# Residual addition from PSUM, and the first ConvFFN weights prepared ahead through DRAM

## The chip, the cores and the metric

The kernel runs on one NeuronCore of a Trainium2 chip. The time is the device time of one execution in microseconds (us). Of several runs the median is given. The profile is of one further execution, and its times count from the first instruction.

## The reference

One layer of a diffusion backbone over 1024 latent tokens and 256 context tokens, 1024 features, all in float32:

```python
hx = modulate(rms_norm(x, norm_pre_mix[l]), sh1, sc1)
fx, ox, zx, gtx, _ = mixer_core(hx, ctx_states, w_in[l], conv_qkv[l], a_log[l], dt_bias[l])
yx = merge_branches(fx, ox, zx, gtx, dn_norm[l], w_fourier[l], w_dn[l], w_out[l])
x = x + gt1 * rms_norm(yx, norm_post_mix[l])
x = ffn_sublayer(x, sh2, sc2, gt2, norm_pre_ffn[l], norm_post_ffn[l], w_up[l],
                 conv_ffn[l], w_down[l], rows, GRID_W)
...
def merge_branches(f_in, o_dn, z, gates, dn_norm, w_fourier, w_dn, w_out):
    ...
    y_f = fourier_mix(f_in) @ w_fourier
    y_d = o @ w_dn
    return (gates[:, :, 0] * y_f + gates[:, :, 1] * y_d) @ w_out

def ffn_sublayer(stream, shift, scale, gate, g_pre, g_post, w_up, conv_w, w_down, rows, cols):
    h = modulate(rms_norm(stream, g_pre), shift, scale)
    a, u = jnp.split(h @ w_up, 2, axis=-1)
    a = dwconv2d(a, conv_w, rows, cols)
    y = (jax.nn.silu(a) * u) @ w_down
    return stream + gate * rms_norm(y, g_post)
```

The change touches the weights of `w_up` and the addition `x + gt1 * rms_norm(yx, ...)`.

## The kernel before

Every float32 product is three matmuls of rounded halves: each operand is split into a rounded part h and a rest l, and h·h, h·l and l·h are summed in PSUM. To split a weight, ScalarE rounds it to h, and VectorE (or, for ConvFFN's weights, POOL) subtracts h from it, which gives l.

The order of the instructions is not that of the source. All operations are recorded, and a list scheduler (`Program.schedule`) sets for each engine and for SP's DMA queue the order of issue, from estimated costs, the longest path behind an operation, and the buffers that its tiles lie in. Every instruction is issued by one helper line, L349. Each engine then goes through its own list in order. A tile waits until the last use of whatever lay in its place before.

The stages around the change, in the times of the profile before:

- Up to 1050, the gates' projection; from there to about 1150 the delta branch's output projection (`for k in range(KT)` over `a["wd"][k]`, 8 steps of 48 matmuls). The weights of a step are two halves of 128x512 (`h_d00`, `h_d0512` and so on), loaded by SP, rounded by ScalarE and split by VectorE. In the same stretch SP loads the last modulation weights (`in_w_ada`).
- To 1201, the Fourier branch's projection, which merges both branches into `mH` and `mL`.
- To about 1300, the output projection by token tiles of 128 rows, the last three of them (5, 6, 7) together. For each tile `root` computes the norm's factor (squares on ScalarE, a power of one column on POOL), `post` scales the two PSUM banks `y2[g]` and adds them to the residual `res`, the sum is stored (`x1d`), normed again and transposed to the hidden state `hh`.
- `side_b` and `sum_b`: ConvFFN's up projection is a scheme of seven products in place of eight over halves of tokens and features. Its moving sides are sums, differences or copies of four parts of `hh`, 28 tiles, each rounded on ScalarE and split on VectorE.
- From 1290 to 1740, the 22 column pairs of the up projection (a pair c has the 128 columns of a and the 128 of u). `both(c)` loads four raw weight halves of 256 KB, makes five sums or differences of them on POOL (`summed`), takes two as they are (`split_w`), and splits all seven: 7 products m1 to m7 of 12 matmuls each. The pools of `wq` hold 5 tiles h, 5 tiles l and 8 raw ones. Products of pairs 0 and 1 are interleaved by a list, later pairs follow one after the other. A pair's result goes into a padded buffer (`apad`, cleared by POOL once), through the 3x3 convolution on VectorE, and to DRAM.
- From 1740, the down projection.

Of the kernel before, what the change touches and what calls it, by code (L numbers as in the profile page):

```python
# [9 lines left out]
F32 = mybir.dt.float32  # L10
# [6 lines left out]
P = 128  # L17
# [470 lines left out]
def layer(prog, a, out):  # L488
# [824 lines left out]
    def m_tile(p_, name, dtype=F32R):  # L1313
        return p_.tile([P, HALF], dtype, tag="m", name=name)
# [55 lines left out]
    def modulation(i):  # L1370
# [8 lines left out]
        for g in range(2):  # L1379
# [11 lines left out]
            else:  # L1391
# [6 lines left out]
                else:  # L1398
                    ve.scalar_tensor_tensor(mod2[:, o0:o0 + 4], pq, 1.0, gpre[:, 8 + g * 4:12 + g * 4],
                                            op0=ALU.add, op1=ALU.mult)  # L1400

    mf = [[m_tile(mp[g], f"mf{k}{g}", F32) for g in range(2)] for k in range(KT)]
    for k in range(KT):
        wl = weights(a["wd"][k], f"d{k}")

        def used(g, hs, pt):
            gl = yt.tile([P, HALF], F32, tag="gl", name=f"g1l{k}{g}")
            sp.dma_start(gl, gd[1, k, :, hs])
            ve.scalar_tensor_tensor(mf[k][g], gl, 1.0, pt, op0=ALU.add, op1=ALU.mult)
        proj_rows(wl, half_rows(oz), f"d{k}", used)  # L1410
        if k % 2:
            modulation(2 + k // 2)
    close(yt)
    close(ozp)

# [48 lines left out]
    def post(y2, res, grow_, name, pl):  # L1464
        r = root(y2, name, pl)
        for g in range(2):
            hs = slice(g * HALF, (g + 1) * HALF)
            t_ = pl.tile([P, HALF], F32, tag="pt", name=f"pt_{name}{g}")
            ve.scalar_tensor_tensor(t_, y2[g], r, grow_[:, hs], op0=ALU.mult, op1=ALU.mult)
            ve.tensor_tensor(res[:, hs], res[:, hs], t_, op=ALU.add)  # L1470


    rings = {1: (mp[0], mp[0]), 3: (lp[0], lp[0]), 4: (mp[1], mp[1]), 2: (lp[1], lp[1])}
# [110 lines left out]

    def both(c):
        raw = {}
        for n, (key, at) in enumerate((("u0", 0), ("u1", 1), ("a0", 0), ("a1", 1))):
            raw[key] = wq.tile([P, HALF], F32, tag="r", name=f"r{key}_{c}", bufs=RAW)
            sp.dma_start(raw[key], a["wu"][c + (NC_FF if key[0] == "u" else 0)][:, at * HALF:(at + 1) * HALF])

        def summed(x_, y_, op, name):
            s_ = wq.tile([P, HALF], F32, tag="l", name=f"qs_{name}{c}", bufs=WL)
            po.tensor_tensor(s_, raw[x_], raw[y_], op=op)
            return split_w(s_, f"{name}{c}")
# [5 lines left out]
        ap_ = apad[c % 2]  # L1600
        inner = lambda g: ap_[:, 1 + 8 * g:9 + 8 * g, 1:GW + 1]
        grid = lambda t_: t_.rearrange("p (a b) -> p a b", b=GW)
        def step(m):
            if m == 2:
                chain(A, summed("u0", "u1", ALU.add, "m2"), 1, True)
                first(lambda: se.activation(v_, A, AF.Copy, scale=-1.0))
            elif m == 5:
                chain(B, summed("a0", "a1", ALU.add, "m5"), 4, True)
                first(lambda: ve.tensor_tensor(v_, v_, B, op=ALU.subtract))
            elif m == 1:  # L1610
                chain(C, summed("a0", "u1", ALU.add, "m1"), 0, True)
                first(lambda: ve.tensor_tensor(v_, v_, C, op=ALU.add))
            elif m == 4:
                chain(A, split_w(raw["u1"], f"m4{c}", True), 3, False)
                first(lambda: se.activation(u_[:, 0:HALF], A, AF.Copy))
            elif m == 3:
                chain(B, split_w(raw["a0"], f"m3{c}", True), 2, False)
                first(lambda: se.activation(inner(1), grid(B), AF.Copy))
            elif m == 7:
                chain(A, summed("a1", "u1", ALU.subtract, "m7"), 6, False)  # L1620
                ve.tensor_tensor(inner(0), grid(A), grid(v_), op=ALU.add)
            else:
                chain(B, summed("u0", "a0", ALU.subtract, "m6"), 5, False)
                ve.tensor_tensor(u_[:, HALF:T], B, v_, op=ALU.add)
# [173 lines left out]
```

## Time and profile before

| | |
|---|---|
| median of 3 runs | 2006.71 us (2005.4 to 2008.88) |
| profiled execution | 2007.74 us |
| its span | 2006.0 us |
| TensorE busy | 1947.3 us, 97% |
| VectorE busy | 1388.3 us, 69% |
| ScalarE busy | 829.7 us, 41% |
| POOL busy | 565.0 us, 28% |
| mean granted TensorE clock | 0.991 |

A row of the profile names the engine (PE is TensorE, PEld its weight loads, DVE VectorE, ACT ScalarE, SPq SP's queue), the operation and its operands: p is PSUM, m SBUF, d DRAM, and in_wu_dram is the input `w_up`; fp32r is the rounded type. Idle time stands with what ended it. A group's mean is over all its instructions.

### The profile page before, as it was taken

Reading aid. Unit: us, or ns where it says so; the run is one execution under the profiler, and the core shown is the slowest. Engines: PE = TensorE matmul, PEld = TensorE weight load, DVE = VectorE, ACT = ScalarE, POOL = GpSimd, SP = SyncE. Lnnn points to the kernel's source line nnn. Section 1 sums busy time; section 2 is a strip of 40 time slices with the busy share of each in tenths; the row PEclk is TensorE's granted clock in tenths of the full one; section 3 lists DMA queues with packets and bytes.
Section 4 is the critical chain, followed back from the end, with each engine's and each line's share of the span. In section 5 each row is a group of like instructions: output and inputs, shape, how many; then the busy total and the mean of one; then the engine's idle time right before and its main releaser. Section 6 shows DMA issues by size and latency. Waiting matters only on the chain.

```text
span 2006.0 us, 31360 instructions
## 1 busy us (share of the span) xinstructions
PE 1947.3 (97%) x11470; PEld 1562.6 (78%) x11470; DVE 1388.3 (69%) x2868; ACT 829.7 (41%) x1948; POOL 565.0 (28%) x573
## 2 busy tenths in 40 slices
PE   7999999999999999999999999989999999999998
PEld 3878888787788887888777778757788888778876
DVE  5659687788678768754656483589988989873132
ACT  5575446455345355333431132444444344622121
POOL 3120121202111122011211000457788888500000
PEclk9999999999999999999999999989999999999999
DMA  7153352544345254233778561312222222543131
GB/s 304 53 193 103 101 156 69 151 142 149 87 135 155 59 168 149 67 104 103 252 254 282 182 216 45 116 44 87 87 83 85 84 75 84 196 156 122 57 126 53
DMA packets 180636, 257.51 MB, mean 128 GB/s; under 512 B 75921, under 2 KB 97522, under 8 KB 180482
## 3 DMA queue, kind: packets, MB, share of 16 engines
q1 hardware_dynamic: 180482, 255.51, 39.5%
q8 instruction: 90, 1.47, 0.3%
q14 instruction: 64, 0.52, 0.1%
HBM read 194.52 MB, written 60.94 MB: 127 GB/s over the span
## 4 chain that ended last, share of the span: by engine, by line
PE 74%; DVE 11%; DMA 5%; ACT 4%; issue 2%; POOL 1%; SPq 0%; DVEq 0%; POOLq 0%; ACTq 0%
PE p L349 74%; DVE m L349 10%; ACT m L349 4%; DMA m<-d 2%; DMA d<-m 2%; DVE p L349 2%; POOL m L349 1%; DMA m<-in_wi_dram 1%; ACT p L349 1%; DMA m<-in_wu_dram 0%; DMA m<-in_w_ada_dram 0%; SPq L349 0%; ACT L349 0%; DVEq L1787 0%; POOLq L1787 0%
## 5 line engine op out<-in xcount | busy, mean ns | idle before, releaser
L349 PE MATMUL p<-m,m 128*128 128x512 f32 (+5 forms) x11310 | 1934.3, 336 | 49.1 <-DVE m L349 17.9
L349 PEld LDWEIGHTS p<-m,m 128*128 128x128 f32 (+3 forms) x11310 | 1544.4, 172 | 429.7 <-issue 53.7
L349 DVE TENSOR_TENSOR m<-m,m 128x512 fp32r<-128x512 f32 (+27 forms) x1116 | 584.1, 539 | 242.6 <-ACT m L349 215.6
L349 ACT ACTIVATE m<-m 128x512 fp32r<-128x512 f32 (+8 forms) x669 | 430.5, 662 | 629.5 <-DMA m<-d 157.4
L349 POOL TENSOR_TENSOR m<-m,m 128x512 fp32r<-128x512 f32 (+5 forms) x338 | 449.8, 1353 | 832.4 <-DVE m L349 672.6
L349 ACT ACTIVATE m<-p 128x512 f32<-128x512 f32 (+4 forms) x510 | 220.9, 447 | 306.9 <-PE p L349 270.2
L349 DVE SCALAR_TENSOR_TENSOR m<-p,m,m 128x128 f32<-128x128 f32 (+4 forms) x488 | 204.0, 452 | 88.4 <-ACT m L349 38.5
L349 DVE SCALAR_TENSOR_TENSOR p<-m,m,p 128x512 f32<-128x512 f32 x352 | 240.1, 749 | 3.5 <-ACT p L349 1.2
L349 ACT ACTIVATE m<-p,m 128x128 f32<-128x128 f32 (+2 forms) x240 | 115.8, 495 | 183.1 <-PE p L349 181.9
L349 POOL MEMSET m<- 128x1024 f32 (+7 forms) x79 | 35.6, 458 | 388.0 <-PE p L349 247.3
L349 POOL COPY m<-m 32x256 f32<-32x256 f32 (+2 forms) x136 | 60.6, 448 | 149.6 <-DMA m<-d 112.2
L349 DVE SCALAR_TENSOR_TENSOR m<-m,m 128x512 f32<-128x512 f32 (+5 forms) x119 | 66.0, 560 | 24.7 <-ACT m L349 19.5
L349 DVE TENSOR_TENSOR m<-p,m 128x512 f32<-128x512 f32 (+4 forms) x91 | 57.6, 644 | 27.9 <-PE p L349 25.7
L349 DVE TENSOR_TENSOR m<-m,p 128x128 f32<-128x128 f32 (+3 forms) x117 | 53.6, 459 | 26.2 <-PE p L349 25.7
L349 DVE COPY m<-p 32x256 f32<-32x256 f32 (+11 forms) x116 | 41.8, 368 | 39.6 <-PE p L349 25.6
L349 DVE SCALAR_TENSOR_TENSOR m<-m,m,m 128x1024 f32<-128x1024 f32 (+2 forms) x68 | 57.9, 855 | 14.0 <-DMA m<-in_w_ada_dram 13.6
L349 ACT ACTIVATE p<-p 128x128 f32<-128x128 f32 x208 | 55.0, 265 | 25.1 <-PE p L349 23.5
L349 DVE SCALAR_TENSOR_TENSOR m<-m,p 128x512 f32<-128x512 f32 x76 | 50.7, 682 | 15.0 <-ACT m L349 7.8
L349 DVE SCALAR_TENSOR_TENSOR m<-m,m,p 128x128 f32<-128x128 f32 x128 | 43.3, 341 | 23.2 <-PE p L349 22.5
L349 DVE SCALAR_TENSOR_TENSOR m<-m 128x1 f32<-128x1 f32 (+1 forms) x25 | 5.4, 217 | 53.8 <-ACT m L349 53.8
L349 ACT ACTIVATION_READ_ACCUMULATOR p<-p 128x1 f32 x208 | 39.5, 190 | 0.0
L349 ACT ACTIVATE p<-m,m 128x512 f32<-128x512 f32 x44 | 30.2, 691 | 21.6 <-DVE m L349 21.3
(20 smaller groups left out, 165.7 us busy)
## 6 DMA issues: line engine op xcount, KB each, us to landing
m<-d SPq DMA_DIRECT2D x76, 512.0 KB
d<-m SPq DMA_DIRECT2D x138, 256.0 KB
m<-d SPq DMA_DIRECT2D x114, 256.0 KB
m<-in_wi_dram SPq DMA_DIRECT2D x106, 256.0 KB
m<-in_w_ada_dram SPq DMA_DIRECT2D x48, 512.0 KB
m<-in_wu_dram SPq DMA_DIRECT2D x88, 256.0 KB
m<-in_wn_dram SPq DMA_DIRECT2D x26, 512.0 KB
m<-d SPq DMA_DIRECT2D x44, 192.0 KB
```

Source lines behind the costliest of these rows:

```text
L349: return getattr(engine.real, method)(*[real(v) for v in args], **{k_: real(v) for k_, v in kw.items()})
```

## The change

It does two things.

First, `post` writes the scaled row back into its PSUM bank `y2[g]` and adds it to the residual from there; the SBUF tile `pt` is gone.

Second, the 14 products' weights of pairs 0 and 1 (`NPRE = 2`) are prepared in the loop of the delta branch's output projection, two in each of the first seven steps: eight raw loads of 256 KB into a pool `pre`, ten sums on POOL, fourteen roundings on ScalarE, fourteen subtractions on POOL, and 28 writes of 256 KB into the DRAM tensor `wsd`. In ConvFFN `ready` then loads h and l from there with 28 loads of 256 KB; the eight raw loads, the sums and the splits of these pairs are no longer made at that place. SP's queue has 56 transfers more.

```diff
--- before.py
+++ after.py
@@ -1399,6 +1399,34 @@
                     ve.scalar_tensor_tensor(mod2[:, o0:o0 + 4], pq, 1.0, gpre[:, 8 + g * 4:12 + g * 4],
                                             op0=ALU.add, op1=ALU.mult)
 
+    NPRE = 2
+    wsd = dram.tile([NPRE, 7, 2, P, HALF], F32, name="wsd")
+    pre = pool("pre", bufs=3, side="right")
+    raws = {}
+    plan = [(c, m) for c in range(NPRE) for m in (2, 4, 5, 3, 1, 7, 6)]
+    parts_of = {2: ("u0", "u1", ALU.add), 5: ("a0", "a1", ALU.add), 1: ("a0", "u1", ALU.add), 4: ("u1",), 3: ("a0",),
+                7: ("a1", "u1", ALU.subtract), 6: ("u0", "a0", ALU.subtract)}
+
+    def raw_of(c, key):
+        if (c, key) not in raws:
+            raws[c, key] = r_ = pre.tile([P, HALF], F32, tag="r", name=f"pr{key}_{c}", bufs=4)
+            at = int(key[1])
+            sp.dma_start(r_, a["wu"][c + (NC_FF if key[0] == "u" else 0)][:, at * HALF:(at + 1) * HALF])
+        return raws[c, key]
+
+    def prepared(c, m):
+        src = raw_of(c, parts_of[m][0])
+        if len(parts_of[m]) > 1:
+            s_ = pre.tile([P, HALF], F32, tag="s", name=f"ps{c}{m}", bufs=2)
+            po.tensor_tensor(s_, src, raw_of(c, parts_of[m][1]), op=parts_of[m][2])
+            src = s_
+        h_ = pre.tile([P, HALF], F32R, tag="h", name=f"ph{c}{m}", bufs=2)
+        se.activation(h_, src, AF.Copy)
+        l_ = pre.tile([P, HALF], F32R, tag="l", name=f"pl{c}{m}", bufs=2)
+        po.tensor_tensor(l_, src, h_.bitcast(F32), op=ALU.subtract)
+        sp.dma_start(wsd[c, m - 1, 0], h_.bitcast(F32))
+        sp.dma_start(wsd[c, m - 1, 1], l_.bitcast(F32))
+
     mf = [[m_tile(mp[g], f"mf{k}{g}", F32) for g in range(2)] for k in range(KT)]
     for k in range(KT):
         wl = weights(a["wd"][k], f"d{k}")
@@ -1410,6 +1438,10 @@
         proj_rows(wl, half_rows(oz), f"d{k}", used)
         if k % 2:
             modulation(2 + k // 2)
+        for _ in range(2):
+            if plan:
+                prepared(*plan.pop(0))
+    close(pre)
     close(yt)
     close(ozp)
 
@@ -1465,9 +1497,8 @@
         r = root(y2, name, pl)
         for g in range(2):
             hs = slice(g * HALF, (g + 1) * HALF)
-            t_ = pl.tile([P, HALF], F32, tag="pt", name=f"pt_{name}{g}")
-            ve.scalar_tensor_tensor(t_, y2[g], r, grow_[:, hs], op0=ALU.mult, op1=ALU.mult)
-            ve.tensor_tensor(res[:, hs], res[:, hs], t_, op=ALU.add)
+            ve.scalar_tensor_tensor(y2[g], y2[g], r, grow_[:, hs], op0=ALU.mult, op1=ALU.mult)
+            ve.tensor_tensor(res[:, hs], res[:, hs], y2[g], op=ALU.add)
 
 
     rings = {1: (mp[0], mp[0]), 3: (lp[0], lp[0]), 4: (mp[1], mp[1]), 2: (lp[1], lp[1])}
@@ -1584,11 +1615,13 @@
 
     def both(c):
         raw = {}
-        for n, (key, at) in enumerate((("u0", 0), ("u1", 1), ("a0", 0), ("a1", 1))):
+        for n, (key, at) in enumerate((("u0", 0), ("u1", 1), ("a0", 0), ("a1", 1)) if c >= NPRE else ()):
             raw[key] = wq.tile([P, HALF], F32, tag="r", name=f"r{key}_{c}", bufs=RAW)
             sp.dma_start(raw[key], a["wu"][c + (NC_FF if key[0] == "u" else 0)][:, at * HALF:(at + 1) * HALF])
 
         def summed(x_, y_, op, name):
+            if c < NPRE:
+                return ready(name)
             s_ = wq.tile([P, HALF], F32, tag="l", name=f"qs_{name}{c}", bufs=WL)
             po.tensor_tensor(s_, raw[x_], raw[y_], op=op)
             return split_w(s_, f"{name}{c}")
@@ -1600,6 +1633,15 @@
         ap_ = apad[c % 2]
         inner = lambda g: ap_[:, 1 + 8 * g:9 + 8 * g, 1:GW + 1]
         grid = lambda t_: t_.rearrange("p (a b) -> p a b", b=GW)
+        def ready(name):
+            hl = [wq.tile([P, HALF], F32R, tag=t_, name=f"q{t_}_{name}{c}", bufs=n) for t_, n in (("h", WH), ("l", WL))]
+            for e, t_ in enumerate(hl):
+                sp.dma_start(t_.bitcast(F32), wsd[c, int(name[1]) - 1, e])
+            return hl
+
+        def plain(key, name):
+            return ready(name) if c < NPRE else split_w(raw[key], f"{name}{c}", True)
+
         def step(m):
             if m == 2:
                 chain(A, summed("u0", "u1", ALU.add, "m2"), 1, True)
@@ -1611,10 +1653,10 @@
                 chain(C, summed("a0", "u1", ALU.add, "m1"), 0, True)
                 first(lambda: ve.tensor_tensor(v_, v_, C, op=ALU.add))
             elif m == 4:
-                chain(A, split_w(raw["u1"], f"m4{c}", True), 3, False)
+                chain(A, plain("u1", "m4"), 3, False)
                 first(lambda: se.activation(u_[:, 0:HALF], A, AF.Copy))
             elif m == 3:
-                chain(B, split_w(raw["a0"], f"m3{c}", True), 2, False)
+                chain(B, plain("a0", "m3"), 2, False)
                 first(lambda: se.activation(inner(1), grid(B), AF.Copy))
             elif m == 7:
                 chain(A, summed("a1", "u1", ALU.subtract, "m7"), 6, False)
```

**POOL, from the output projection's last tiles to the second pairs.** Before; the operations on 128x1 are the power of `root`, `m_11115<-m_11074,m_11072` is the first sum of pair 0, and `m_11133<-m_11072,m_11127` the l of its product m4:

```order
L349 TENSOR_TENSOR m_10742<-m_10742,m_62 128x1
L349 TENSOR_TENSOR m_11115<-m_11074,m_11072 128x512
L349 TENSOR_TENSOR m_11133<-m_11072,m_11127 128x512
L349 TENSOR_TENSOR m_11145<-m_11064,m_11062 128x512
L349 TENSOR_TENSOR m_10643<-m_10643,m_62 128x1
L349 TENSOR_TENSOR m_11160<-m_11107,m_11101 128x512
L349 TENSOR_TENSOR m_11170<-m_11115,m_11141 128x512
L349 TENSOR_TENSOR m_11183<-m_11160,m_11173 128x512
L349 TENSOR_TENSOR m_11195<-m_11101,m_11149 128x512
```

Now; `m_11524` and `m_11596` are the two padded buffers, `m_11550`, `m_11206` and `m_11581` the first sum, l and the next sum of pair 2:

```order
L349 TENSOR_TENSOR m_10759<-m_10759,m_62 128x1
L349 TENSOR_TENSOR m_10794<-m_10794,m_62 128x1
L349 TENSOR_TENSOR m_10825<-m_10825,m_62 128x1
L349 MEMSET m_11524 128x1188
L349 TENSOR_TENSOR m_11550<-m_11211,m_11195 128x512
L349 TENSOR_TENSOR m_11206<-m_11550,m_11190 128x512
L349 TENSOR_TENSOR m_11581<-m_11230,m_11195 128x512
L349 MEMSET m_11596 128x1188
L349 TENSOR_TENSOR m_11169<-m_11581,m_11157 128x512
```

The 24 operations of pairs 0 and 1 are gone from here, and the power operations are followed at once by the clearing of the buffers and pair 2. They stand now among the delta branch's four operations on 128x1024, ahead of the first power.

**ScalarE, where the delta branch's output projection begins.** Before; `m_497<-m_342` is the first half of d1, `m_9587<-m_9562` its second, `m_479<-m_318` the first half of d0 and `m_490<-m_331` its second; `m_9559` is a weight of the output projection, and the operations from p are gates:

```order
L349 ACTIVATE m_497<-m_342 128x512
L349 ACTIVATE m_9559<-m_9528 128x1024
L349 ACTIVATE m_9052<-p_173 128x512
L349 ACTIVATE m_9587<-m_9562 128x512
L349 ACTIVATE m_479<-m_318 128x512
L349 ACTIVATE m_9068<-p_124 128x512
L349 ACTIVATE m_9052<-p_126 128x512
L349 ACTIVATE m_9068<-p_167 128x512
L349 ACTIVATE m_490<-m_331 128x512
```

Now; `m_9552` and `m_9566` are the two buffers of prepared weights' h:

```order
L349 ACTIVATE m_9552<-m_9525 128x512
L349 ACTIVATE m_497<-m_342 128x512
L349 ACTIVATE m_9566<-m_9554 128x512
L349 ACTIVATE m_9054<-p_173 128x512
L349 ACTIVATE m_9603<-m_9570 128x512
L349 ACTIVATE m_9566<-m_9587 128x512
L349 ACTIVATE m_479<-m_318 128x512
L349 ACTIVATE m_9070<-p_124 128x512
L349 ACTIVATE m_9552<-m_9539 128x512
L349 ACTIVATE m_9054<-p_126 128x512
L349 ACTIVATE m_9070<-p_167 128x512
L349 ACTIVATE m_490<-m_331 128x512
```

Four roundings of pair 0 stand among the four halves of d0 and d1, and the output projection's weight has gone to a later place. In SP's queue the writes stand between the loads of the branch's next weights in the same way.

## Rows read from the trace of the kernel before

**Rows 1.** Busy time of each engine by stage: us, then TensorE, its loads, VectorE, ScalarE, POOL, ...
```profile
1040.00:1140.00 100.00, 99.82 (x413) 73.50 (x412) 55.18 (x69) 14.50 (x23) 9.59 (x4) 1.00 0.71 237
...
1287.40:1303.00 15.60, 13.52 (x55) 10.00 (x53) 8.50 (x11) 6.20 (x17) 11.16 (x11) 0.89 0.17 69
1303.00:1346.00 43.00, 33.32 (x122) 22.70 (x121) 36.91 (x40) 22.85 (x39) 23.20 (x16) 0.87 0.16 51
1346.00:1361.50 15.50, 12.89 (x52) 9.98 (x50) 13.92 (x20) 5.54 (x10) 12.74 (x11) 0.93 0.10 35
1361.50:1448.50 87.00, 83.31 (x358) 67.96 (x358) 85.38 (x121) 37.28 (x65) 67.73 (x51) 0.97 0.28 94
1448.50:1456.00 7.50, 7.46 (x22) 5.99 (x23) 5.84 (x9) 3.46 (x7) 3.25 (x3) 0.63 0.18 69
1456.00:1740.00 284.00, 283.80 (x1252) 234.35 (x1251) 250.31 (x347) 125.47 (x211) 234.16 (x177) 1.00 0.25 85
```

**Rows 2.** Groups of VectorE from 1302 to 1346: count, busy us, mean ns, idle before.
```profile
L349 DVE TENSOR_TENSOR m<-m,m 128x512 fp32r<-128x512 f32 x20 | 18.7, 951 | 6.5 <-ACT m L349 6.5
L349 DVE TENSOR_TENSOR m<-m,m 128x512 f32<-128x512 f32 x16 | 17.2, 1078 | 1.1 <-ACT m L349 0.6
L349 DVE TENSOR_TENSOR m<-m,p 128x512 f32<-128x512 f32 x4 | 2.7, 683 | 1.2 <-PE p L349 1.1
```

**Rows 3.** Groups of POOL from 1281 to 1346, same columns.
```profile
L349 POOL TENSOR_TENSOR m<-m,m 128x512 fp32r<-128x512 f32 x15 | 23.4, 1579 | 14.0 <-ACT m L349 12.4 <-DMA m<-in_wu_dram 1.6
L349 POOL TENSOR_TENSOR m<-m,m 128x512 f32<-128x512 f32 x10 | 14.4, 1446 | 7.8 <-PE p L349 7.8
```

**Rows 4.** Timeline of VectorE from 1303: start, us, count, [idle before <- releaser].
```profile
1306.51 0.69 DVE L349 TENSOR_TENSOR m<-m,m 128x512 fp32r<-128x512 f32 x1 [6.46 <-ACT m L349]
...
1344.59 1.18 DVE L349 TENSOR_TENSOR m<-m,m 128x512 fp32r<-128x512 f32 x1
...
1350.91 1.41 DVE L349 SCALAR_TENSOR_TENSOR p<-m,m,p 128x512 f32<-128x512 f32 x2 [1.01 <-ACT p L349]
```

**Rows 5.** Timeline of all engines from 1281, same columns.
```profile
1286.81 3.39 DVE L349 TENSOR_TENSOR m<-m,m 128x512 f32<-128x512 f32 x2
...
1292.65 10.52 PE L349 MATMUL p<-m,m 128*128 128x512 f32 x38 [2.05 <-ACT m L349]
...
1294.29 2.27 DVE L349 TENSOR_TENSOR m<-m,m 128x512 f32<-128x512 f32 x2
```

**Rows 6.** Chain of waits from 1150 to 1480: start us, us, what ran or was waited for.
```profile
1275.12 0.43 SPq L349
...
1276.55 5.27 DMA m<-in_wu_dram
...
1358.32 2.51 POOL m L349 x2
...
1361.53 44.38 PE p L349 x187
```

**Rows 7.** Groups of VectorE from 1200 to 1250.
```profile
L349 DVE SCALAR_TENSOR_TENSOR m<-p,m,m 128x512 f32<-128x512 f32 x8 | 5.6, 746 | 2.7 <-POOL m L349 2.7
L349 DVE TENSOR_TENSOR m<-m,m 128x512 f32<-128x512 f32 x8 | 5.1, 683 | 0.0
```

**Rows 8.** The page's costliest groups: the one of VectorE that reads and writes PSUM.
```profile
L349 DVE SCALAR_TENSOR_TENSOR p<-m,m,p 128x512 f32<-128x512 f32 x352 | 240.1, 749 | 3.5 <-ACT p L349 1.2
```

**Rows 9.** Groups of ScalarE from 1265 to 1346: the roundings.
```profile
L349 ACT ACTIVATE m<-m 128x512 fp32r<-128x512 f32 x35 | 21.1, 640 | 26.5 <-DVE m L349 14.3 <-POOL m L349 6.5 <-PE p L349 5.7
```

**Rows 10.** Two slices of 10 us of the delta branch's projection, columns of rows 1.
```profile
1060.00:1070.00 10.00, 10.00 (x44) 8.02 (x43) 4.59 (x7) 0.63 (x1) 2.40 (x1) 1.00 0.95 330
...
1120.00:1130.00 10.00, 10.00 (x45) 7.59 (x44) 1.55 (x3) 1.26 (x2) 0.00 (x0) 1.00 0.19 53
```

**Rows 11.** What SP's queue waited for from 1040 to 1140: us, times, longest us.
```profile
SPq L349 <- DVE m L349: 28.3, 26, 4.1
SPq L349 <- PE p L349: 26.2, 15, 4.9
```

## Prediction

> **What bounds the kernel now.** I read the busy time by stage first, then the timeline of VectorE, the groups of VectorE and POOL, and the chain of waits.
>
> In the windows [rows 1], TensorE is all but full while the delta branch is projected (99.82 of 100 us, 1040 to 1140) and again in the long ConvFFN stretch from 1456: 284 us for 1252 matmuls, 0.2268 us each at a granted clock of 1.00. Between them, from 1287.4 to 1361.5, stand 55 + 122 + 52 = 229 matmuls. [...] From 1361.5 to 1456, 380 matmuls need 86.2 us and take 94.5: 8.3 us more, behind VectorE (85.38 of 87 us busy there).
>
> What holds the first stretch? VectorE builds there the sides of ConvFFN's products from the hidden state. Its timeline [rows 4] shows no pause that matters between 1306.51 and 1345.77, when the last side is ready; it had waited 6.46 us for the first one before that, and the convolution's first product runs at 1350.91. Its groups [rows 2] show why it takes so long: 20 subtractions of 951 ns on average and 16 sums of 1078 ns, although the same operation in the same shape takes 683 ns while POOL has no weights in hand [rows 7]. POOL does 25 weight operations of 1446 to 1579 ns in the same stretch [rows 3], and both read SBUF. The four VectorE subtractions that read one side from PSUM stayed at 683 ns [rows 2]. The excess is 20 x 0.268 + 16 x 0.395 = **11.7 us**. The same is seen on the residual's additions of token tiles 6 and 7: two took 3.39 us and two 2.27 us [rows 5] in place of 1.37, 2.9 us more, and TensorE stood 2.05 us behind the hidden state. The chain of waits [rows 6] goes just this way: a raw weight that lands 5.27 us after its issue, and later two operations on POOL at 1358.32, behind which TensorE starts pair 3 at 1361.53.
>
> **The change, part by part.**
>
> *The addition from PSUM.* The scaled row goes back to its bank, and the addition reads SBUF and PSUM instead of SBUF twice. Scaling to SBUF took 746 ns, an operation of that kind that writes PSUM 749 [rows 7, 8]; adding took 683 ns with two SBUF inputs [rows 7] and 683 with one in PSUM [rows 2]. I book 0 for the 16 pairs of operations by themselves. The edit only takes the additions of token tiles 6 and 7 out of POOL's way, which the other part does as well. [...]
>
> *What leaves the stretch after 1278.* Fourteen subtractions and ten sums on POOL, fourteen roundings on ScalarE of 640 ns [rows 9] and eight raw loads. The order on POOL shows that between the last root and the clearing of the second padded buffer nothing is left, and that the clearing is followed by three operations of pair 2 before the first buffer is cleared. So VectorE meets POOL in two or three operations at the end of its sides and no more. Worked out for the moment the last side is ready (1345.77): 2.9 us from the additions of token tiles 6 and 7, 1.1 us of the 2.05 us gap with its slow matmuls behind it, 11.7 us of the excess, 1.2 us of VectorE's waits for products [rows 2], less 2 us for what POOL still does there: **15 us earlier**. The clearing of the first padded buffer waits for the last side, and from it to the first weight of pair 3 POOL's chain is as long as before (1345.77 to 1361.53, 15.8 us), with one subtraction less ahead of it: 16 us earlier. For this, TensorE has to put 229 matmuls into 58 us, 6 more than full clock needs. The convolution starts as much earlier; the stretch to 1456 is bound by VectorE, keeps its length and its 8.3 us, and behind it TensorE is full to 1740, so nothing is given back. **Term: -16 us.** Its bounds: 0, if the weights hold it as before, and -22, the whole loss.
>
> *What takes its place.* 28 loads of 256 KB in place of eight, straight into the weights' slots. Such a load, queued behind others, landed 5.27 us after its issue [rows 6]. The slots of five products are filled ahead; of the later loads the tightest, by TensorE's order, has 17 matmuls, 3.9 us, between the last use of its slot and its own first use, and would be 1.4 us late if it were queued like that one. DMA was busy for 0.10 to 0.17 of that time [rows 1], so I book 0 and keep 1.4 us as the upper end.
>
> *What the delta branch's projection gets.* POOL: 24 operations of at most 1.58 us, 36 us of a span where it was busy for 10 of 100 us [rows 1]. VectorE, which meets them, has 45 us free; if each of 24 meetings costs a microsecond it is at 79 of 100. ScalarE: 14 x 0.64 = 9 us on top of 14.5. SP: 36 more transfers at 0.43 us [rows 6], 15.5 us, in a queue that spends 28.3 + 26.2 us waiting for VectorE and TensorE to free buffers [rows 11]. DMA is the tight one: 237 GB/s over 100 us [rows 1] are 23.7 MB, the 36 transfers add 36 x 0.262 = 9.4 MB, and 33.1 MB at the 330 GB/s of its fullest slice (busy 0.95 [rows 10]) are 100 us out of 100. What saves it: the prepared pool lies where later stages' buffers do, so an out-projection weight and the first rows of x (0.5 MB each) are loaded after it, and the load was uneven (0.19 busy at 1120 to 1130 [rows 10]). On ScalarE, the order shows four roundings of prepared weights among the branch's first four weight halves; the third of them fills the second's buffer again, so it waits until that one's write has landed, and d0's first half stands right behind it. TensorE is full there, so the bounds are 0 (nothing to gain in 0.18 us of idle time) and 5.27 us for one write's landing that all stand behind. I take **+1 us**, near the lower end: only the first weights of the branch are used soon after their rounding, the later ones are prepared most of a step (48 matmuls, 10.9 us) ahead.
>
> **Sum:** -16 + 1 = -15. The profiled execution took 2007.74 us (its span is 2006.0), so 1992.7; the median of the three runs shown, 2006.71, is 1.0 us less, and I forecast **1992 us** for the median. No change, as a measurement of this kernel can tell it, is within 0.2%, 4 us.
>
> **The rivals.**
>
> *Half of it (2000 us).* VectorE gets through its sides 15 us earlier, but the weights of pairs 2 and 3, still made on POOL, or the loads from DRAM, then arrive after TensorE is ready. For it: POOL's order keeps the clearing of the first buffer behind the last side, ahead of these weights, and they get their slots only as products end. Against it: DMA is nearly idle there, and the chain on POOL is the one of before. If three loads are late by 1.4 us each and POOL's chain by three operations of 1.45 us [rows 3], 8.5 us are given back: -16 + 8.5 + 1 = -6.5.
>
> *Slower (2013 us).* The roundings, 12 of 14 of which need an earlier write to have landed, stand in ScalarE's queue ahead of the branch's weights, and DMA is full. If in each of the eight steps one weight half comes late by half a queued landing, 2.6 us, TensorE loses 21 us, and 21 - 16 + 1 = +6. It decides from a lateness of 2 us a step (8 x 2 = 16). For it: the 100 of 100 us of DMA. Against it: weights are most of a step ahead, and DMA had a slice at 0.19.
>
> *No change (2006 us).* The stretch after 1361.5 is VectorE's, 85.38 of 87 us. If its convolutions meet more POOL work once pairs 2 and 3 come closer, 14 meetings of 1 us give the gain back. Against it: its POOL work (67.73 us) is the same.
>
> *More (1984 us).* The stall ahead of 1456 goes too, since VectorE starts its convolutions with a lead over TensorE: -16 - 8.3 + 1 = -23. Against it: both start earlier by about the same.
>
> [...]
>
> **How the numbers follow.** Forecast 0.62 (its own range 1987 to 1997), half 0.13, more 0.11, no change 0.06, slower 0.08. Faster by over 0.2% are the first three: 0.86; the same 0.06; slower 0.08. The range runs from 1984 (the case of more) to 2004 (half, with the d loop's 5.27 us in full), and leaves out about 0.15.
>
> **What would show it.** Right: in the windows, 0.95 or more of TensorE's time busy from 1287 to the end of pair 1; VectorE's sides at 690 to 760 ns on average; the last side at about 1331; TensorE's matmul of pair 3 at about 1346; DMA busy over 0.85 from 1050 to 1120 with TensorE still over 98 of 100. Wrong: TensorE waiting for ScalarE or VectorE in the branch's projection for more than 5 us, or for loads from DRAM after 1290.

## The result, and the profile after

The changed kernel took **1993.28 us**, median of 4 runs (1991.62 to 1997.87), against 2006.06 us for the kernel before, run beside it 4 times. The ratio of the two kernels over these executions is 0.9931, with a 95% interval of 0.9912 to 0.9951, that is 10 to 18 us less (the quotient of the two medians is 0.9936). On another chip, later, it was 0.9927 (0.9901 to 0.9953). The forecast was 1992 us, in a range of 1984 to 2004. The profiled execution took 1991.62 us against 2007.74, 16.1 us less.

The windows of the changed kernel, with the edges and columns of [rows 1] (after the POOL column come the granted TensorE clock, the busy share of DMA, and GB/s):

```profile
1040.00:1140.00 100.00, 98.37 (x407) 72.35 (x406) 56.91 (x64) 22.17 (x36) 47.92 (x28) 1.00 0.94 320
...
1287.40:1303.00 15.60, 14.85 (x75) 11.59 (x73) 5.10 (x10) 7.79 (x17) 1.65 (x3) 1.00 0.58 197
1303.00:1346.00 43.00, 35.50 (x153) 26.71 (x151) 38.94 (x57) 20.50 (x35) 16.83 (x13) 1.00 0.26 88
1346.00:1361.50 15.50, 14.83 (x52) 11.60 (x53) 14.85 (x22) 6.52 (x12) 7.31 (x6) 0.79 0.15 51
1361.50:1448.50 87.00, 84.36 (x367) 68.22 (x367) 84.44 (x119) 39.17 (x68) 70.31 (x53) 1.00 0.28 92
1448.50:1456.00 7.50, 7.50 (x35) 6.21 (x34) 7.45 (x12) 2.40 (x6) 5.93 (x5) 1.00 0.44 139
1456.00:1740.00 284.00, 281.58 (x1238) 231.60 (x1237) 254.66 (x352) 132.83 (x216) 222.37 (x168) 1.00 0.30 103
```

From 1040 to 1140 POOL now works 47.92 us in place of 9.59 and DMA is busy for 0.94, and TensorE still for 98.37 of 100 us. VectorE's splits of 128x512, those of the delta branch's weights above all, are what now meets POOL. Their group in this window, before and in the change:

```profile
L349 DVE TENSOR_TENSOR m<-m,m 128x512 fp32r<-128x512 f32 x17 | 12.4, 727 | 16.5 <-ACT m L349 16.3
L349 DVE TENSOR_TENSOR m<-m,m 128x512 fp32r<-128x512 f32 x16 | 18.0, 1130 | 12.1 <-ACT m L349 11.9
```

So the lengthening did not vanish, it moved: from 727 to 1130 ns here, where VectorE is busy for 56.91 of 100 us and has room for it. The first scaling of `post` starts at 1210.75 before and at 1210.92 now, so the whole gain lies behind it. From 1287 to 1303 the clock stays at 1.00 and TensorE has little idle time. Between 1346 and 1361.5 the clock is lower than before (0.79 against 0.93).

How far TensorE got by a given time is read from the groups of its full matmuls. Of the kernel before, from 1287.4 to 1361.5:

```profile
L349 PE MATMUL p<-m,m 128*128 128x512 f32 x193 | 56.8, 448 | 10.6 <-ACT m L349 7.1 <-DVE m L349 3.3
L349 PE MATMUL p<-m,m 128*128 128x128 f32 x32 | 5.3, 283 | 1.2 <-ACT m L349 1.2
```

And of the changed kernel, the same stretch:

```profile
L349 PE MATMUL p<-m,m 128*128 128x512 f32 x246 | 63.4, 410 | 8.8 <-ACT m L349 7.7 <-DVE m L349 1.1
```

That is 53 matmuls of 512 columns more by 1361.5; at 0.2268 us, 12.0 us. The windows from there to 1456 hold 367 + 35 = 402 against 380, 5.0 us more. Together they are 17 us, and 16.1 us is what the spans differ by. How they divide into 12 and 5 depends on the edge at 1361.5: TensorE's wait for pair 3, with slow matmuls behind it, falls on it before (pair 3 starts at 1361.53 [rows 6]) and well ahead of it now (1346.24, below). The clock just behind these two starts, first before, then in the change:

```profile
1361.50:1366.00 4.50, 4.47 (x12) 3.35 (x13) 4.41 (x8) 2.64 (x5) 1.79 (x2) 0.62 0.15 58
1346.00:1350.00 4.00, 3.33 (x7) 2.23 (x8) 4.00 (x7) 3.28 (x6) 1.28 (x1) 0.50 0.00 0
1350.00:1353.00 3.00, 3.00 (x9) 2.34 (x9) 2.93 (x5) 0.00 (x0) 0.00 (x0) 0.57 0.23 87
```

In slices of 0.25 us the granted clock reads 0.50 or 1.00 here, but for the slices in which it changes; behind the two starts it is at 0.50 for about 3.4 us before and 6.6 us now. (The group of the kernel before also corrects the forecast's bound of -22 for this stretch. That bound sets 52 us, 229 matmuls of 0.2268 us, against the 74.1 us of the stretch; 32 of the 229 were transposes of 128 columns, so more than 22 us had been lost there.)

The groups of VectorE in the stage of the sides, 1300 to 1347, to be held against [rows 2]:

```profile
L349 DVE TENSOR_TENSOR m<-m,m 128x512 fp32r<-128x512 f32 x20 | 14.3, 741 | 5.1 <-ACT m L349 4.9
L349 DVE TENSOR_TENSOR m<-m,m 128x512 f32<-128x512 f32 x16 | 12.9, 825 | 2.6 <-ACT m L349 2.3
```

The same 36 operations take 27.2 us in place of 35.9. The subtractions are at 741 ns, the sums at 825, in place of 951 and 1078. On the timeline, the residual's additions of token tiles 6 and 7, now with one side in PSUM, stand against [rows 5]:

```profile
1285.10 1.28 DVE L349 TENSOR_TENSOR m<-m,p 128x512 f32<-128x512 f32 x2
...
1290.98 1.27 DVE L349 TENSOR_TENSOR m<-m,p 128x512 f32<-128x512 f32 x2
...
1291.52 8.66 PE L349 MATMUL p<-m,m 128*128 128x512 f32 x38 [0.69 <-ACT m L349]
```

Each pair takes 1.28 us, where it had taken 3.39 and 2.27, and TensorE's wait for the hidden state fell from 2.05 to 0.69 us.

VectorE's timeline has the first operation on the sides, the last two, and the convolution's first products, against [rows 4]:

```profile
1301.01 0.69 DVE L349 TENSOR_TENSOR m<-m,m 128x512 fp32r<-128x512 f32 x1 [4.93 <-ACT m L349]
...
1330.75 1.28 DVE L349 TENSOR_TENSOR m<-m,m 128x512 fp32r<-128x512 f32 x2
...
1336.61 8.66 DVE L349 SCALAR_TENSOR_TENSOR p<-m,m,p 128x512 f32<-128x512 f32 x13 [0.82 <-ACT p L349]
```

The first side starts 5.5 us earlier, the last is ready at 1332.0, 13.7 us earlier, and the convolution runs 14.3 us earlier. From the first side's start to the last one's end it takes 31.0 us in place of 39.3.

POOL's timeline of the changed kernel:

```profile
1321.85 1.10 POOL L349 MEMSET m<- 128x1188 f32 x1 [27.86 <-ACT m L349]
1324.38 1.29 POOL L349 TENSOR_TENSOR m<-m,m 128x512 f32<-128x512 f32 x1 [1.43 <-PE p L349]
```

Its queue stands for 27.86 us at the first clearing of a buffer, and works on pair 2 only afterwards. TensorE, on its timeline from 1328, meets the end of that chain:

```profile
1333.87 9.37 PE L349 MATMUL p<-m,m 128*128 128x512 f32 x40 [1.89 <-ACT m L349]
1346.24 1.22 PE L349 MATMUL p<-m,m 128*128 128x512 f32 x2 [3.01 <-ACT m L349]
```

Pair 3 starts at 1346.24, 15.3 us earlier than in [rows 6], after a wait of 3.01 us. It stands at the same place of TensorE's order in both kernels, so this is a lead of 15.3 us in the same work. In the stretch ahead of 1456 TensorE had a wait of 3.70 us before, with the slow matmuls of [rows 1] behind it; now a shorter one stands at another place, at a clock of 1.00. First before, then the change:

```profile
1448.54 13.68 PE L349 MATMUL p<-m,m 128*128 128x512 f32 x48 [3.70 <-DVE m L349]
1414.54 19.73 PE L349 MATMUL p<-m,m 128*128 128x512 f32 x84 [1.97 <-DVE m L349]
```

### The profile page after: what moved, and what is told of

Its sections match the earlier page's. It is cut to its first block, busy times and chain, and to the rows that moved or that the text cites. A ratio compares the mean times of both kernels' runs of the same rounds, so it can differ in the third digit from the quotient of the medians.

```text
span 1989.9 us, 31477 instructions
## 1 busy us (share of the span) xinstructions
PE 1934.6 (97%) x11470; PEld 1556.4 (78%) x11470; DVE 1379.6 (69%) x2868; ACT 831.4 (42%) x1948; POOL 568.7 (29%) x573
## 4 chain that ended last, share of the span: by engine, by line
PE 74%; DVE 13%; DMA 5%; ACT 4%; issue 2%; POOL 0%; SPq 0%; DVEq 0%; POOLq 0%; ACTq 0%
PE p L349 74%; DVE m L349 10%; ACT m L349 3%; DVE p L349 3%; DMA d<-m 2%; DMA m<-d 2%; ACT p L349 0%; POOL m L349 0%; DMA m<-in_w_ada_dram 0%; DMA m<-in_wi_dram 0%; DMA m<-in_cf_dram 0%; SPq L349 0%; ACT L349 0%; DVEq L1829 0%; POOLq L1829 0%
## 5 line engine op out<-in xcount | busy, mean ns | idle before, releaser
L349 DVE TENSOR_TENSOR m<-m,m 128x512 fp32r<-128x512 f32 (+26 forms) x1100 | 568.7, 532 | 239.7 <-ACT m L349 210.7
L349 DVE SCALAR_TENSOR_TENSOR m<-p,m,m 128x128 f32<-128x128 f32 (+4 forms) x472 | 192.5, 441 | 83.0 <-ACT m L349 39.1
L349 DVE TENSOR_TENSOR m<-m,p 128x128 f32<-128x128 f32 (+3 forms) x133 | 63.7, 485 | 22.9 <-PE p L349 22.1
L349 DVE SCALAR_TENSOR_TENSOR m<-m,m,m 128x1024 f32<-128x1024 f32 (+2 forms) x68 | 59.1, 873 | 13.2 <-DMA m<-in_w_ada_dram 12.8
```

The source lines that it names most:

```text
L349: return getattr(engine.real, method)(*[real(v) for v in args], **{k_: real(v) for k_, v in kw.items()})
```

## The experiments

The theory: POOL's operations on the first two pairs' weights read SBUF beside VectorE's operations with two SBUF inputs and lengthen these; taking them away shortens the sides, and TensorE follows. The rivals: the addition from PSUM does it; the chain from raw load to split does it; any work on POOL does it. The ratios are each against the kernel before on the same chip. The last column is the time in each profile from the first scaling of `post` to the end of the last side. It is counted from there because the stages ahead don't come out alike, the planner (`Program.schedule`) making a new order for every edit: the first scaling starts at 1210.75 before and at 1210.92 in the change, but at 1213.1 in run 7 and at 1218.4 in run 5, which differ from these two in no operation ahead of it. The same kernel gives the same offset (1217.5 in run 6, 1216.6 in run 11). A ratio therefore holds some microseconds that the edit's own stage did not cause, and the last two columns say more about the cause than the ratio does.

| run | ratio, 95% interval | subtractions, sums of the sides (mean ns) | first scaling to last side (us) |
|---|---|---|---|
| before | 1 | 951, 1078 | 135.0 |
| the change | 0.9931 (0.9912 to 0.9951) | 741, 825 | 121.1 |
| 1 addition alone | 0.9986 (0.9977 to 0.9994) | 1075, 1033 | 133.3 |
| 2 preparation alone | 0.9921 (0.9909 to 0.9933) | 820, 787 | 123.1 |
| 3 preparation, unused | 0.9990 (0.9978 to 1.0002) | 1151, 1003 | 133.7 |
| 4 POOL busy, reading | 0.9983 (0.9970 to 0.9995) | 970, 1144 | 130.3 |
| 5 POOL busy, not reading | 0.9913 (0.9898 to 0.9928) | 686, 693 | 117.2 |
| 6 change, splits on POOL | 0.9921 (0.9908 to 0.9934) | 741, 825 | 121.1 |
| 7 before, splits on POOL | 0.9974 (0.9962 to 0.9987) | 951, 1070 | 133.1 |
| 8 three pairs | 0.9957 (0.9943 to 0.9970) | 686, 688 | 118.0 |
| 9 the change again | 0.9927 (0.9901 to 0.9953) | 740, 825 | 121.2 |
| 10 as 6, clearing on VectorE | 0.9912 (0.9883 to 0.9940) | 836, 788 | 123.6 |
| 11 as 6, again | 0.9910 (0.9885 to 0.9936) | 739, 826 | 121.1 |
| 12 one pair | 0.9967 (0.9949 to 0.9985) | 875, 956 | 126.0 |

**1. The addition alone.** The kernel before, with this edit of `post`:

```diff
-            t_ = pl.tile([P, HALF], F32, tag="pt", name=f"pt_{name}{g}")
-            ve.scalar_tensor_tensor(t_, y2[g], r, grow_[:, hs], op0=ALU.mult, op1=ALU.mult)
-            ve.tensor_tensor(res[:, hs], res[:, hs], t_, op=ALU.add)
+            ve.scalar_tensor_tensor(y2[g], y2[g], r, grow_[:, hs], op0=ALU.mult, op1=ALU.mult)
+            ve.tensor_tensor(res[:, hs], res[:, hs], y2[g], op=ALU.add)
```

> The addition from PSUM alone, weights as before. Contention theory (POOL's operations on the first two pairs' weights hold up VectorE's operations with two SBUF inputs): only the additions of token tiles 6 and 7 get out of POOL's way, 2.9 us at most; they return to 0.7 us each, the last side is ready at 1342 to 1345, the time falls by 0 to 4 us. Rival (the addition is what matters): 8 us or more. [...]

Its additions of tiles 6 and 7 on VectorE's timeline:

```profile
1290.20 1.28 DVE L349 TENSOR_TENSOR m<-m,p 128x512 f32<-128x512 f32 x2
...
1296.23 1.27 DVE L349 TENSOR_TENSOR m<-m,p 128x512 f32<-128x512 f32 x2
```

They are out of POOL's way at once, 1.28 us a pair, while POOL still makes weights. The time fell by 0.14%, 2.8 us, as the theory had it. But the last side came at 1347.5, not between 1342 and 1345: the sides themselves are no shorter than before (1075 and 1033 ns), since POOL's work was there still. Counted from the first scaling the last side came 1.7 us sooner, and from there to the end this profile is 6.0 us shorter than that of before, with the wait ahead of 1456 shorter without an edit there. So the gain in time can't be put down to the additions alone.

**2. The preparation alone.** The change, with the edit above taken back.

> The weights prepared ahead alone, the addition from an SBUF tile as before. Contention theory: with no weight work on POOL beside them, the additions of tiles 6 and 7 take 0.7 us each from SBUF too, the last side is ready at about 1332, pair 3 starts at about 1346, the time is 10 to 16 us under that of before, as with the whole change. Rival (the addition matters): under 6 us.

The additions of tiles 6 and 7, now from SBUF, with no weights on POOL beside them:

```profile
1287.37 1.28 DVE L349 TENSOR_TENSOR m<-m,m 128x512 f32<-128x512 f32 x2
...
1293.09 1.28 DVE L349 TENSOR_TENSOR m<-m,m 128x512 f32<-128x512 f32 x2
```

The same 1.28 us a pair as from PSUM. The ratio (0.9921) can't be told from that of the whole change. The last side came at 1336.0 and pair 3 at 1348.1, later than the 1332 and 1346 expected, in a profile whose first scaling came 2.1 us late. So the preparation carries the gain, and beside it the addition from PSUM adds nothing that these times can tell. The rival falls.

**3. The preparation, unused.** The change, with `both` making all weights from raw loads again (its three conditions on `NPRE` taken out).

> The preparation runs in the delta branch's projection and is written to DRAM, but the two pairs' weights are then made from raw loads as before, so nothing is gained later. This prices the preparation by itself. Forecast's term: +1 us, from 0 to 5.3; the trace of the changed kernel suggests 0.2 (the delta branch's last matmul ended 0.23 us later than before). Rival (a large price hidden inside a larger gain): +4 us or more, with TensorE waiting in the projection.

Against run 1, which has the addition from PSUM too, the ratio is 0.0004 higher, 0.8 us; by the two intervals this is uncertain by some 3 us. TensorE in its window:

```profile
1040.00:1140.00 100.00, 98.20 (x405) 72.55 (x405) 57.76 (x63) 22.18 (x36) 47.60 (x28) 1.00 0.94 318
```

With DMA busy for 0.94 and POOL for 47.6 us, TensorE is busy for 98.20 of 100 us. From 1000 to 1170 it waited for 1.7 us, against 0.8 in run 1. So the preparation costs about 1 us, as the forecast had it; a price of 4 us or more, with TensorE waiting in the projection, is not there.

**4. POOL busy beside the sides, reading.** The change, and in `ready`, behind the loads:

```diff
+            for _ in range(2 + (name[1] in "25")):
+                po.tensor_tensor(idle, hl[0].bitcast(F32)[:, 0:384], hl[1].bitcast(F32)[:, 0:384], op=ALU.subtract)
```

> The whole change, and POOL gets 32 subtractions of 128x384 that read the two halves of each prepared weight after it has landed; nothing waits for their results. Weights come from DRAM as in the change, only the contention is put back. Contention theory: VectorE's side operations lengthen again to about 0.9 us on average, the last side moves from 1332 to 1339 to 1345, the time is 6 to 13 us above the changed kernel's. Rival (the chain load, sum, rounding, split on the way to the weights was what cost): within 3 us of the changed kernel.

VectorE's two groups, 1300 to 1347:

```profile
L349 DVE TENSOR_TENSOR m<-m,m 128x512 fp32r<-128x512 f32 x20 | 18.7, 970 | 4.6 <-ACT m L349 4.5
L349 DVE TENSOR_TENSOR m<-m,m 128x512 f32<-128x512 f32 x16 | 17.9, 1144 | 1.5 <-ACT m L349 1.2
```

and POOL's group of the added subtractions:

```profile
L349 POOL TENSOR_TENSOR m<-m,m 128x384 f32<-128x384 f32 x19 | 22.7, 1196 | 11.3 <-DMA m<-d 10.3
```

Nothing waits for these subtractions, the weights still come from DRAM, and yet the operations on the sides are as long as before the change, the last side comes at 1344.1 (1339 to 1345 was expected), and most of the gain is gone (0.9983, 10 us above the change). This is the contention by itself. The chain of sums, roundings and splits isn't needed to explain the loss, and neither are the loads, which are those of the change.

**5. POOL busy, but not reading two tiles.** In place of these subtractions, clearings:

```diff
+            po.tensor_copy(idle[:, 0:1], hl[0].bitcast(F32)[:, 0:1])
+            for _ in range(5 + (name[1] in "25")):
+                po.memset(idle, 0.0)
```

> As the run with POOL kept busy beside the sides, but POOL clears a tile of 128x384 (5 or 6 times for each prepared product, released by a copy of one column of its weight) and so is busy without reading two tiles. Theory that POOL's reading is what blocks VectorE: VectorE's side operations stay near 0.7 us, the last side is ready at most 3 us after that of the change. Rival (any POOL work beside VectorE, or its place in the queue, costs as much): means of 0.9 us and more, last side 9 us later as in that run. The clearings also stand ahead of pair 2's weights in POOL's queue, so pair 3 can start late in both; the time decides less than the means.

VectorE's same groups, 1300 to 1347:

```profile
L349 DVE TENSOR_TENSOR m<-m,m 128x512 fp32r<-128x512 f32 x20 | 13.5, 686 | 6.3 <-ACT m L349 6.2
L349 DVE TENSOR_TENSOR m<-m,m 128x512 f32<-128x512 f32 x16 | 11.1, 693 | 0.6
```

and POOL's group of the added clearings:

```profile
L349 POOL MEMSET m<- 128x384 f32 x42 | 18.5, 440 | 2.2
```

POOL is about as busy as in run 4 (28.5 against 29.5 us of these 47), and VectorE's operations are at 686 and 693 ns, shorter than in the change, whose POOL had begun pair 2. The last side came at 1335.6, 3.6 us behind that of the change where 3 were allowed, but this profile was 7.5 us late already at the first scaling; counted from there it is 3.9 us sooner. So it is POOL's reading that lengthens VectorE's operations, not its being busy. VectorE's four operations with one side in PSUM stayed at 680 ns in the same stretch of run 4, as they had at 683 before the change [rows 2]. The time was as low as the best here (0.9913). The planner also set another order on TensorE, and its timeline from 1330 shows what came of that:

```profile
1329.85 45.40 PE L349 MATMUL p<-m,m 128*128 128x512 f32 x194 [0.33 <-DVE m L349]
```

194 matmuls run without a gap, where the change waits 3.01 us for pair 3. In the change, as before it, two matmuls of pair 3's first product stand in TensorE's order ahead of 60 of pair 2's 84; here 16 are left. That order alone, without the clearings, wasn't tried.

**6 and 7. The four early splits on POOL.** In the middle of the up projection VectorE also makes the first four splits of the down projection. The edit, once on the change and once on the kernel before:

```diff
-            ve.tensor_tensor(gl, gf, gh.bitcast(F32), op=ALU.subtract)
+            (po if blk == 0 and c < 4 else ve).tensor_tensor(gl, gf, gh.bitcast(F32), op=ALU.subtract)
```

> The whole change, and the first four splits for the down projection (128x384, made in the middle of the up projection) go from VectorE to POOL. In the trace of the change they take VectorE 1.65 us each between 1400 and 1424, and TensorE then waits 2.0 us at 1412 and runs short again at 1434. Theory (VectorE's backlog there is the four splits): the two waits go, 2 to 4 us less than the change. Rival (POOL, 8 of 10 us busy there, becomes late with weights): no change or slower.

> The kernel before, with the same four splits on POOL. Before, three of them run back to back just ahead of the wait of 3.7 us at 1444.8, after which TensorE runs at the lower clock for some 5 us. Theory (part of the change's gain, about 3 us, came from the splits falling into another place, not from the weights): 5 to 8 us less than before, so that what the change is worth beside it falls from 16 to about 13. Rival (the stall follows from the late start of the stage): 0 to 2 us.

The window from 1400 to 1460, before:

```profile
1400.00:1460.00 60.00, 56.30 (x236) 45.81 (x236) 55.84 (x77) 24.54 (x43) 46.52 (x35) 0.94 0.27 90
```

of the change:

```profile
1400.00:1460.00 60.00, 57.59 (x251) 46.40 (x250) 56.64 (x77) 24.83 (x43) 48.74 (x36) 1.00 0.25 83
```

of run 6:

```profile
1400.00:1460.00 60.00, 60.00 (x266) 49.70 (x265) 55.10 (x80) 27.77 (x48) 53.16 (x41) 1.00 0.27 93
```

and of run 7:

```profile
1400.00:1460.00 60.00, 60.00 (x265) 49.47 (x264) 57.27 (x82) 25.16 (x45) 53.41 (x41) 1.00 0.28 95
```

TensorE issues 236 matmuls there before, 251 in the change, 266 and 265 with the splits on POOL, which is 60 us at full clock. So the stall ahead of 1456 belongs to these splits on VectorE. The kernel before gains 0.26% by it alone (0.9974), 5 us, the least of what was expected. With the splits out of the way on both sides, the change's worth is 0.9921 against 0.9974, about 11 us, or 13 us by run 11's 0.9910; with the splits on VectorE on both sides it is 14 to 15 us (0.9931 and 0.9927). Each of these is uncertain by some 4 to 6 us, so the times don't show that a part of the gain came from where the splits fell. The traces show that the stall shrank with the change, and no run separates what that part is worth.

**8. Three pairs.** `NPRE = 3`, and three products in a step.

> Three pairs prepared, three products in each of seven steps. Theory: POOL has nothing left between the clearing of the buffers and pair 3, whose first weight then waits for no chain: TensorE's wait of 3.2 us ahead of pair 3 and the slow matmuls behind it go, 4 to 6 us. Against it 21 transfers more, 5.5 MB, in a projection whose DMA was busy for 0.94: 38 MB at 349 GB/s are 109 us, so 3 to 9 us more there. Together -3 to +4 us against the change. Rival (DMA has room in later stages for what is pushed out): -4 us or better.

What TensorE waited for from 1000 to 1170 (us, times, longest us), first in the change:

```profile
PE p L349 <- DVE m L349: 1.5, 2, 0.8
```

and in run 8:

```profile
PE p L349 <- ACT m L349: 4.7, 4, 2.7
PE p L349 <- DVE m L349: 1.8, 2, 1.2
```

The waits in the gates' and the delta branch's projection grow to 6.5 us, and the window from 1000 to 1060 shows a granted clock below 1:

```profile
1000.00:1060.00 60.00, 57.17 (x235) 43.85 (x233) 32.24 (x38) 17.69 (x30) 14.91 (x10) 0.97 0.77 250
1040.00:1140.00 100.00, 96.07 (x398) 71.73 (x397) 59.50 (x60) 24.12 (x40) 61.77 (x38) 1.00 0.93 325
```

The wait for pair 3 didn't go either; the timeline from 1344 has it still, and POOL's first sum of pair 3 ahead of it:

```profile
1352.72 1.26 POOL L349 TENSOR_TENSOR m<-m,m 128x512 f32<-128x512 f32 x1 [10.54 <-PE p L349]
1354.70 0.73 PE L349 MATMUL p<-m,m 128*128 128x512 f32 x2 [2.06 <-ACT m L349]
```

It fell by only 1 us, though POOL had no chain ahead of it: POOL now waits 10.54 us for TensorE to free the slot of the sum. The ratio is 0.9957, 5 us worse than the change. The profile shows both sides of the account. The first scaling of run 8 starts at 1222.9, 12.0 us later than in the change; TensorE's longer waits above are 5.0 us of that. From there its last side comes 3.1 us sooner than in the change, with the sides at 686 and 688 ns, and 3.1 us is also what it gains to the end: the third pair did bring some 3 of the 4 to 6 us expected, and the projection cost more. Two pairs fit into the delta branch's projection, three don't. This is the forecast's rival "slower", one pair further on, and more than was expected of it here; by the code the third pair adds 18 transfers and not 21. ScalarE's waits for writes to land, the mechanism of that rival, grow with it: from 1020 to 1110 they are 4.8 us before, 22.3 in the change and 31.0 in run 8.

**9 to 11. The change beside two versions of it.** Run 9 is the change, run 11 is run 6 again; run 10 clears the two buffers on VectorE besides:

```diff
     for t_ in apad:
-        po.memset(t_, 0.0)
+        ve.memset(t_, 0.0)
```

> The changed kernel once more, on the same chip as the three that follow: 11 to 17 us under the kernel before, as measured first.

> The change with the four splits on POOL, and the two buffers cleared on VectorE. In the change POOL's queue waits 28 us, from 1294 to 1322, at the clearing of the first buffer, and pair 2's weights stand behind it; TensorE later waits 3.2 us ahead of pair 3, and its matmuls then go at the lower clock. Theory (the clearings at POOL's head are what makes pair 3 late): that wait goes, 3 to 7 us less than with the splits alone, though VectorE has two clearings of about 1 us more. Rival (pair 2's weights wait for their slots, not for POOL): within 2 us of it, or slower, as POOL's earlier work meets VectorE's sides again.

> The change with the four splits on POOL once more, beside the change on the same chip: 1 to 4 us less than the change.

Medians of six runs on one chip: 1994.48 us (1991.22 to 1997.22) for the change, 1990.23 (1988.90 to 1994.00) with the splits on POOL, 1990.19 with the clearing on VectorE too. The change repeats, and with the splits on POOL it is 4.3 us faster beside it, a little more than expected, in six runs of each that overlap. The clearing's place brings nothing more, and POOL's timeline of run 10 says why:

```profile
1327.65 1.29 POOL L349 TENSOR_TENSOR m<-m,m 128x512 f32<-128x512 f32 x1 [31.28 <-PE p L349]
```

Without a clearing at its head POOL waits as long, 31.28 us, but now for TensorE: pair 2's first sum needs a slot whose weight product m7 of pair 0 still uses. Pair 3 starts after 2.51 us of waiting:

```profile
1348.54 1.17 PE L349 MATMUL p<-m,m 128*128 128x512 f32 x2 [2.51 <-ACT m L349]
```

So the rival held: the slots set when POOL can begin pair 2, and the clearing only stood where POOL would have waited anyway.

**12. One pair.** `NPRE = 1`.

> Only pair 0 prepared ahead. Twelve of the 24 operations stay on POOL beside the sides, so by the contention theory about half of the lengthening stays: side operations at 0.85 to 0.95 us on average, the last side at 1337 to 1341, the time 6 to 11 us under that of before. Rival (the first pair's weights alone open the stage): the whole gain, 13 us or more.

VectorE's two groups, 1300 to 1347:

```profile
L349 DVE TENSOR_TENSOR m<-m,m 128x512 fp32r<-128x512 f32 x20 | 17.0, 875 | 5.5 <-ACT m L349 5.4
L349 DVE TENSOR_TENSOR m<-m,m 128x512 f32<-128x512 f32 x16 | 15.1, 956 | 2.6 <-ACT m L349 2.3
```

They lie about halfway between before and the change (911 ns over all 36, the last side at 1337.3, both as expected), and so does the time (0.9967, 6.6 us). With none, one and two pairs prepared the gain grows with the number of operations taken from POOL, as the contention theory has it; the first pair alone doesn't open the stage.

## Why the prediction was right

- *What bounds the stage.* Right. Runs 4, 5 and 12 show that the length of the operations on the sides follows POOL's reading, by itself and in about the proportion of POOL's operations (1007, 911 and 778 ns over the 36 with none, one and two pairs prepared). Of the signs named for being right, three came: the last side, pair 3, and a DMA share over 0.85 with TensorE busy for 98.37 of 100 us. Two did not. The sides stayed at 741 and 825 ns, not at 690 to 760, since POOL's work on pair 2 met their end: an excess of 3.4 us, counted as in the forecast, where 2 had been allowed. And TensorE was busy for 0.90 and not 0.95 of the time from 1287.4 to 1341, by when its order has done with pair 1.
- *The addition from PSUM by itself: 0.* Right with the rest of the change in place (runs 1 and 2): no price, at 1.28 us a pair from PSUM and from SBUF, and no gain that could be told. Alone the time fell by 2.8 us, as much as the forecast had put on the additions of tiles 6 and 7, but run 1 doesn't show that it is theirs.
- *The stage: -16 us.* The last side was forecast at about 1331 and came at 1332.0, the convolution 15 us earlier and it was 14.3, pair 3 at about 1346 and it was 1346.24, 15.3 us earlier. The parts were less even. The first side started 5.5 us earlier, where 2.9 + 1.1 = 4.0 had been worked out, and from it to the end of the last one 8.3 us were saved, where 11.7 + 1.2 - 2 = 10.9 had been. The two differences partly cancel.
- *The stretch to 1456 "keeps its length and its 8.3 us".* Right in its length and wrong in its parts. From 15.3 us at pair 3's first matmul the lead grew only to the 16.1 us of the spans. But TensorE was at a clock of 0.50 for about 6.6 us behind the wait for pair 3, in place of 3.4, and against that its wait of 3.70 us with the slow matmuls behind it (a clock of 0.63 from 1448.5 to 1456 [rows 1]) became one of 1.97 us without. By the granted clock the first cost about 1.6 us more and the second gave some 4 us; neither was foreseen. The splits for the down projection, which no step of the forecast named, fell into other places: what was wrong is the step that took VectorE's backlog there for the convolution's alone, and the stall that went is a part of the rival "more". That so little of these shifts was left is luck.
- *The loads from DRAM: 0.* Right. What TensorE waited for in the change from 1287.4 to 1361.5 was ScalarE (7.7 us) and VectorE (1.1 us) alone, as its group above shows.
- *The preparation: +1 us.* Right: about 1 us in run 3, at a DMA share of 0.94. VectorE's bound of 79 of 100 us was far off: no run shows the microsecond that it takes for each of 24 meetings, and VectorE is busy for 56.91, though its splits there lengthened from 727 to 1130 ns. That ScalarE's roundings wait for writes to land came true (22.3 us from 1020 to 1110) and didn't reach TensorE, which waited for 1.5 us. How near the edge this is, run 8 shows.
- *The sum.* -16.1 us in the profile where -15 was forecast; the medians differ by 12.8 us, and the interval of 10 to 18 us holds all three. The runs of one kernel spread over 6 us and more here, and the planner's other orders move a profile by up to 7.5 us, so that the sum agrees to 1 us is luck in part. The windows and the runs confirm the mechanism, not the last microsecond.

## What to carry to other kernels

Where an engine off the critical path works in SBUF beside the one on it, look at the same operation's mean time with and without that work: the difference times the count is what moving it can take off that engine, and it can be read before the change is made (here 11.7 us, of which 8.3 came). Move such work to a stage that is bound by something else, here matrix products: it lengthens the same operations there too (from 727 to 1130 ns), but the engine has room (busy for 56.91 of 100 us). Check by bytes over time that its DMA traffic still fits there, since one pair more was already too much (run 8, 0.9957). An in-order queue that stands for long at one instruction (27.86 us here) is not proof that the instruction is in the way: see what the next one would have waited for (31.28 us in run 10). Where a planner sets the order, compare a stage from a landmark ahead of it in each profile, and not by the whole time alone.

## What the runs showed of the hardware

Beside POOL's clearings VectorE's 36 operations on the sides took 689 ns on average (run 5), against 683 ns with no weights on POOL [rows 7]; beside its subtractions they took 1047 ns (run 4), half as long again. VectorE's additions with one side in PSUM took 1.28 us a pair while POOL was reading (run 1), as they did in the change. And with DMA busy for 0.94 over 100 us, at 320 GB/s, with writes and reads of 256 KB mixed in one queue, TensorE waited for no more than 1.5 us.
